# A first feed-forward product with Strassen's seven products on three of eight row-block pairs

## Chip, cores and metric

The kernel runs on one core of one Trainium2 chip. The metric is device time in microseconds (us), the median of several runs. A profiled execution has a span of its own, which is shown beside the median.

## What is computed

One layer of a streaming encoder over 256 tokens of width 2048, in float32. The change concerns the feed-forward part, the product before it (`merged @ w_o`) and the one behind it (`w_ple_gate`). D_FF is 5632.

```python
def reference(x, p, g_mix, w_in, ..., w_o, g_ffn, w_ffn_in, w_ffn_out, g_ple, w_ple_gate, w_ple_proj, g_final):
    ...
        x = x + merged @ w_o[i]

        h = rms_norm(x, g_ffn[i])
        a, b = jnp.split(h @ w_ffn_in[i], 2, axis=-1)
        x = x + (jax.nn.silu(a) * b) @ w_ffn_out[i]

        ple_gate = jax.nn.sigmoid(rms_norm(x, g_ple[i]) @ w_ple_gate[i])
        x = x + ple_gate * (p[i] @ w_ple_proj[i])
    return rms_norm(x, g_final)
```

## The kernel before

The 256 tokens are two token tiles t of 128 partitions (NT = 2, P = 128, S = 256). Each product of the layer is a stream of weight tiles from HBM. `load` (L170) has SyncE (SP) fetch four row blocks of 128 by 512 columns, 1 MB, into a `raw` tile. `split` (L185) makes of each half of it, 128x1024, a high part in the matmul's reduced float32 form on ScalarE (`hi`, L191) and the rest on VectorE (`lo`, L192). `products` (L196) then adds three matmuls of 128x512 on TensorE: high by high (L200), high by low (L201), low by high (L202). The activations on the other side are held transposed, split the same way by `transposed_split` (L144): transposes on TensorE (L137), high part on ScalarE (L152, or L159 with a gain), low part on VectorE (L153, L160).

`project` (L204) is the loop: it takes two PSUM banks, one for each token tile, and goes over the row blocks in groups of four: 24 matmuls for each group, and after each group `group_done` lets work start that was put off with `later`, so that transposes come some 24 matmuls after their inputs.

The feed-forward part is: for each of 11 blocks n of 512 columns, `fa` (the first half of w_ffn_in, 96 matmuls), its gate with sigmoid on ScalarE (L553) and a multiplication on VectorE (L554), `fb` (the second half, 96 matmuls), and the second multiplication (L559) that gives `sa`; its transposes, `aT`, come 24 matmuls into the next block. After all 11 blocks the second product `fo` runs in four column blocks over all 44 row blocks of `aT`, 264 matmuls each, and its two banks are added to x1 (L578). Ahead of it `wo` ends in the additions at L537; `pg` (w_ple_gate) comes behind it.

Order within an engine is set by the scheduler from the program's text; buffers come from pools that live as long as the kernel: `blk` (36 tiles), `raw` (4), `split` (3 pairs), and 4 + 4 PSUM banks. Since the pools are shared, loads and splits of the next product run ahead of the end of the one before.

## Time and profile before

| | |
|---|---|
| median of 3 runs | 2221.39 us (2221.09 to 2222.83) |
| span of the profiled execution | 2220.6 us |
| TensorE busy | 2205.8 us, 99% of the span |
| VectorE busy | 1222.5 us, 55% |
| ScalarE busy | 975.4 us, 44% |
| first feed-forward product (fa, fb) | 1378.9 to 1867.4 us of the span |
| second (fo) | 1867.4 to 2110.6 us |

In the profile PE is TensorE's matmuls, PEld its weight loads, DVE VectorE, ACT ScalarE, SPq the queue of SyncE, which issues the loads. A matmul's record (about 390 ns) is longer than the distance of two matmuls, since they are pipelined; the distance is what counts for time. PEclk is the granted clock of TensorE, 1.00 for 2.4 GHz and 0.50 for 1.2 GHz.

### The profile page before, as it was taken

The numbers are of one execution on the slowest core, as the hardware profiler recorded it, in microseconds if no ns is written. First come the engines' busy times: TensorE is split into PE (matmuls) and PEld (weight loads), VectorE is DVE, ScalarE is ACT, GpSimd is POOL, SyncE is SP. The second block draws the span as 40 slices with busy tenths as digits, with TensorE's granted clock in tenths as the row PEclk, the third lists the DMA queues.
The fourth block names the chain that finished last, engine by engine and source line by source line (L and its number), as shares of the span: only waits on it lengthen the run. The fifth ranks groups of instructions, "written<-read, shape, count | busy, mean of one in ns | idle before, by whom it ended". The sixth has DMA issues, their size and how long they took to land.

```text
span 2220.6 us, 24771 instructions
## 1 busy us (share of the span) xinstructions
PE 2205.8 (99%) x10054; PEld 1834.0 (83%) x10054; DVE 1222.5 (55%) x1347; ACT 975.4 (44%) x1101; POOL 9.4 (0%) x19
## 2 busy tenths in 40 slices
...
GB/s 263 187 189 190 189 189 190 195 199 193 174 190 182 181 179 186 178 178 180 177 190 189 190 209 205 185 190 192 191 184 191 191 190 183 196 194 191 191 195 128
DMA packets 229106, 420.05 MB, mean 189 GB/s; under 512 B 7424, under 2 KB 42368, under 8 KB 228992
## 3 DMA queue, kind: packets, MB, share of 16 engines
...
## 4 chain that ended last, share of the span: by engine, by line
PE 99%; DMA 0%; ACT 0%; issue 0%; DVE 0%; SPq 0%; ACTq 0%; POOLq 0%
PE fo_ps L201 4%; PE fa_ps L202 4%; PE fa_ps L201 4%; PE fa_ps L200 4%; PE fo_ps L202 4%; PE fb_ps L200 4%; PE fo_ps L200 4%; PE fb_ps L202 4%; PE fb_ps L201 4%; PE v_ps L202 3%; PE v_ps L201 3%; PE v_ps L200 3%; PE g_ps L202 3%; PE g_ps L201 3%; PE g_ps L200 3%; PE qk_ps L201 3%
## 5 line engine op out<-in xcount | busy, mean ns | idle before, releaser
L192 DVE TENSOR_TENSOR fo_lo<-fo_raw,fo_hi 128x1024 fp32r<-128x1024 f32 x88 | 107.8, 1225 | 123.5 <-ACT fo_hi L191 123.5
L192 DVE TENSOR_TENSOR fa_lo<-fa_raw,fa_hi 128x1024 fp32r<-128x1024 f32 x88 | 107.8, 1225 | 111.4 <-ACT fa_hi L191 111.4
L192 DVE TENSOR_TENSOR fb_lo<-fb_raw,fb_hi 128x1024 fp32r<-128x1024 f32 x88 | 107.8, 1225 | 110.8 <-ACT fb_hi L191 110.8
L191 ACT CAST fa_hi<-fa_raw 128x1024 fp32r<-128x1024 f32 x88 | 92.8, 1054 | 142.8 <-PE fa_ps L202 87.9
L191 ACT CAST fo_hi<-fo_raw 128x1024 fp32r<-128x1024 f32 x88 | 92.8, 1055 | 137.4 <-PE fo_ps L202 132.4
L191 ACT CAST fb_hi<-fb_raw 128x1024 fp32r<-128x1024 f32 x88 | 92.7, 1053 | 121.9 <-PE fb_ps L202 85.3
L201 PE MATMUL fo_ps<-fo_lo,aT_hi 128*128 128x512 f32 x352 | 137.1, 389 | 0.0
L202 PE MATMUL fa_ps<-fa_hi,h2T_lo 128*128 128x512 f32 x352 | 137.0, 389 | 0.0
L201 PE MATMUL fa_ps<-fa_lo,h2T_hi 128*128 128x512 f32 x352 | 137.0, 389 | 0.0
L202 PE MATMUL fo_ps<-fo_hi,aT_lo 128*128 128x512 f32 x352 | 137.0, 389 | 0.0
L201 PE MATMUL fb_ps<-fb_lo,h2T_hi 128*128 128x512 f32 x352 | 136.9, 389 | 0.0
L202 PE MATMUL fb_ps<-fb_hi,h2T_lo 128*128 128x512 f32 x352 | 136.9, 389 | 0.0
L200 PE MATMUL fa_ps<-fa_hi,h2T_hi 128*128 128x512 f32 x352 | 127.2, 392 | 0.0
L200 PE MATMUL fo_ps<-fo_hi,aT_hi 128*128 128x512 f32 x352 | 124.4, 390 | 0.0
L192 DVE TENSOR_TENSOR ro_lo<-ro_raw,ro_hi 128x1024 fp32r<-128x1024 f32 x64 | 78.4, 1225 | 83.0 <-ACT ro_hi L191 83.0
L200 PE MATMUL fb_ps<-fb_hi,h2T_hi 128*128 128x512 f32 x352 | 122.6, 389 | 0.0
L191 ACT CAST g_hi<-g_raw 128x1024 fp32r<-128x1024 f32 x64 | 67.2, 1050 | 109.8 <-PE g_ps L202 81.9
L191 ACT CAST v_hi<-v_raw 128x1024 fp32r<-128x1024 f32 x64 | 67.4, 1054 | 106.3 <-PE v_ps L202 53.3
L192 DVE TENSOR_TENSOR v_lo<-v_raw,v_hi 128x1024 fp32r<-128x1024 f32 x64 | 78.3, 1224 | 62.4 <-ACT v_hi L191 62.4
L191 ACT CAST ro_hi<-ro_raw 128x1024 fp32r<-128x1024 f32 x64 | 67.5, 1054 | 102.3 <-PE ro_ps L202 98.9
L192 DVE TENSOR_TENSOR qk_lo<-qk_raw,qk_hi 128x1024 fp32r<-128x1024 f32 x64 | 78.3, 1224 | 61.0 <-ACT qk_hi L191 61.0
L192 DVE TENSOR_TENSOR g_lo<-g_raw,g_hi 128x1024 fp32r<-128x1024 f32 x64 | 78.3, 1224 | 60.4 <-ACT g_hi L191 60.4
(241 smaller groups left out, 5467.9 us busy)
## 6 DMA issues: line engine op xcount, KB each, us to landing
fa_raw<-in_w_ffn_in_dram SPq DMA_DIRECT2D x44, 1024.0 KB, 4.9
fb_raw<-in_w_ffn_in_dram SPq DMA_DIRECT2D x44, 1024.0 KB, 4.9
fo_raw<-in_w_ffn_out_dram SPq DMA_DIRECT2D x44, 1024.0 KB, 5.0
qk_raw<-in_w_in_dram SPq DMA_DIRECT2D x64, 512.0 KB, 4.3
v_raw<-in_w_in_dram SPq DMA_DIRECT2D x32, 1024.0 KB, 5.0
g_raw<-in_w_in_dram SPq DMA_DIRECT2D x32, 1024.0 KB, 4.8
ro_raw<-in_w_ret_out_dram SPq DMA_DIRECT2D x32, 1024.0 KB, 5.0
cv_raw<-in_w_in_dram SPq DMA_DIRECT2D x16, 1024.0 KB, 4.9
```

The costliest lines, as they stand in the source:

```text
L191: last_copy[0] = nc.scalar.copy(out=hi, in_=raw[:, h0 : h0 + 2, :])
L192: nc.vector.tensor_tensor(out=lo, in0=raw[:, h0 : h0 + 2, :], in1=hi.bitcast(F32), op=ALU.subtract)
L200: nc.tensor.matmul(out=ps, lhsT=xh[:, ts], rhs=wh, start=first, stop=False)
L201: nc.tensor.matmul(out=ps, lhsT=xh[:, ts], rhs=wl, start=False, stop=False)
L202: nc.tensor.matmul(out=ps, lhsT=xl[:, ts], rhs=wh, start=False, stop=last)
```

## The change

The first product is written on pairs of row blocks. For row blocks (2i, 2i + 1), the two token tiles and the two column blocks (the `a` one and the `b` one of n) form a product of 2x2 blocks. `FAST` marks three of the eight pairs, 0, 2 and 4, for which it is done by Strassen's scheme in Winograd's form with seven block products; the other five take the plain eight. Each block product is three matmuls as before. All pairs add into the same banks P1 to P7 (the plain ones into P2 to P5), so that the scheme's closing additions are done once for each n, in `product_pair`, on VectorE. The sums on the activations' side are made once, by `pair_forms`, while `wo` runs; those on the weights' side for each fast pair: three operations on VectorE (L639, L645, L646 of the changed kernel), and then high and low parts of three blocks (1536 columns) and of four sums (2048 columns) by `halves_of` (L214 on ScalarE, L215 on VectorE).

As seven banks are taken, the second product can't wait for the end of the first with banks of its own: after every second block n it adds those two blocks' share to x1 (L742, 48 additions in all, for 8 before); the last part holds block 10 alone. The pools are closed and opened twice: ahead of the first product (`stage.open(mixed=True)`: 11 `blk`, 3 `raw`, 1 `sums`, 6 `parts` of 2048 columns, 8 PSUM banks in one pool) and behind the second. What lives across is in `keep` (20 tiles).

Counted in the built program, 9237 matmuls have 512 columns, 9336 before; those with fewer are as many as before.

```diff
+    class Stage:
+        def open(self, mixed, blks=17):
+            stage_pools.close()
+            self.mixed = mixed
+            def pool(name, bufs, **space):
+                return stage_pools.enter_context(
+                    tc.tile_pool(name=f"{name}{int(mixed)}", bufs=bufs, reuse_waits="tile", **space)
+                )
+            self.blk = pool("blk", 11 if mixed else blks)
+            if mixed:
+                self.raw = pool("raw", 3)
+                self.sums = pool("sums", 1)
+                self.parts = pool("parts", 6)
+                self.mm = self.aux = pool("ps", 8, space=PSUM)
+            else:
+                self.raw = pool("raw", 4)
+                self.split = pool("split", 3)
+                self.mm = pool("ps_mm", 4, space=PSUM)
+                self.aux = pool("ps_aux", 4, space=PSUM)
+    stage = Stage()
+    stage.open(mixed=False)
...
+    def halves_of(src, j0, jn, name):
+        hi, lo = (stage.parts.tile([P, 4, W], F32R, tag="part", name=f"{name}_{x}") for x in ("hi", "lo"))
+        last_copy[0] = nc.scalar.copy(out=hi[:, :jn, :], in_=src[:, j0 : j0 + jn, :])
+        nc.vector.tensor_tensor(
+            out=lo[:, :jn, :], in0=src[:, j0 : j0 + jn, :], in1=hi[:, :jn, :].bitcast(F32), op=ALU.subtract
+        )
+        return hi, lo
...
+        if stage.mixed:
+            hi, lo = halves_of(raw, 0, kn, name)
+            return [(hi[:, j, :], lo[:, j, :]) for j in range(kn)]
...
+    def pair_forms(src, j0, fast, name, gain):
+        pt = transposed(src, j0, f"{name}_t")
+        a = blk([P, 2, S], F32, f"{name}_a")
+        for j in range(2):
+            g = gains[:, gain + j0 + j : gain + j0 + j + 1]
+            nc.scalar.activation(out=a[:, j, :], in_=pt[:, j, :], func=AF.Copy, scale=g)
+        main = keep([P, 2, 2, S], F32R, f"{name}_f")
+        nc.scalar.copy(out=main[:, 0], in_=a)
+        nc.vector.tensor_tensor(out=main[:, 1], in0=a, in1=main[:, 0].bitcast(F32), op=ALU.subtract)
+        t1, t2 = slice(0, P), slice(P, 2 * P)
+        n = 4 if fast else 2
+        mix = blk([P, n, P], F32, f"{name}_m")
+        if fast:
+            a11, a12, a21, a22 = a[:, 0, t1], a[:, 1, t1], a[:, 0, t2], a[:, 1, t2]
+            stt = nc.vector.scalar_tensor_tensor
+            stt(out=mix[:, 0, :], in0=a21, scalar=-1.0, in1=a22, op0=ALU.mult, op1=ALU.subtract)
+            stt(out=mix[:, 1, :], in0=mix[:, 0, :], scalar=-1.0, in1=a11, op0=ALU.mult, op1=ALU.subtract)
+            nc.vector.tensor_tensor(out=mix[:, 2, :], in0=a11, in1=a21, op=ALU.subtract)
+            nc.vector.tensor_tensor(out=mix[:, 3, :], in0=a12, in1=mix[:, 1, :], op=ALU.subtract)
+        else:
+            nc.vector.tensor_tensor(out=mix, in0=a[:, :, t1], in1=a[:, :, t2], op=ALU.subtract)
+        more = keep([P, 2, n, P], F32R, f"{name}_d")
...
+    FAST = (True, False, True, False, True, False, False, False)
+    def product_pair(lhs, w, c1, c2, name):
+        banks, left = {}, {}
+        for p in range(1, 8):
+            plain = {2: 1, 3: 1, 4: 1, 5: 1}.get(p, 0)
+            left[p] = sum(3 if f else 6 * plain for f in FAST)
+        total = dict(left)
+        def add(p, stat, mov):
+            if p not in banks:
+                banks[p] = stage.mm.tile([P, W], F32, tag="ps", name=f"{name}_p{p}")
+            (xh, xl), (wh, wl) = stat, mov
+            for x, y in ((xh, wh), (xh, wl), (xl, wh)):
+                nc.tensor.matmul(out=banks[p], lhsT=x, rhs=y, start=left[p] == total[p], stop=left[p] == 1)
+                left[p] -= 1
+        c = [blk([P, NT, W], F32, f"{name}_c{i}") for i in range(2)]
+        keep_ps = blk([P, 2, W], F32, f"{name}_k")
+        us = blk([P, 2, W], F32, f"{name}_u")
+        p1, p5 = keep_ps[:, 0, :], keep_ps[:, 1, :]
+        tt = nc.vector.tensor_tensor
+        for i, fast in enumerate(FAST):
+            rows = w[2 * i * P : 2 * (i + 1) * P, :].rearrange("(c p) n -> p c n", p=P)
+            raw = stage.raw.tile([P, 4, W], F32, tag="raw", name=f"{name}_raw{i}")
+            nc.sync.dma_start(out=raw[:, 1:3, :], in_=rows[:, :, c1 : c1 + W])
+            nc.sync.dma_start(out=raw[:, 0:4:3, :], in_=rows[:, :, c2 : c2 + W])
+            if fast:
+                hi, lo = halves_of(raw, 1, 3, f"{name}_b{i}")
+                b = {k: (hi[:, j, :], lo[:, j, :]) for j, k in enumerate((1, 2, 3))}
+                sums = stage.sums.tile([P, 4, W], F32, tag="sums", name=f"{name}_s{i}")
+                tt(
+                    out=sums[:, 0:2, :],
+                    in0=raw[:, 1:4:2, :],
+                    in1=raw[:, 0:1, :].broadcast_to([P, 2, W]),
+                    op=ALU.subtract,
+                )
+                tt(out=sums[:, 2, :], in0=raw[:, 3, :], in1=sums[:, 0, :], op=ALU.add)
+                tt(out=sums[:, 3, :], in0=raw[:, 2, :], in1=sums[:, 2, :], op=ALU.subtract)
+                hi, lo = halves_of(sums, 0, 4, f"{name}_t{i}")
+                b |= {k: (hi[:, j, :], lo[:, j, :]) for j, k in enumerate((5, 7, 6, 4))}
+                for p in (1, 2, 3, 6, 7, 4, 5) if i == 0 else (1, 6, 7, 4, 5, 3, 2):
+                    add(p, lhs[i][p], b[p])
+            else:
+                hi, lo = halves_of(raw, 0, 4, f"{name}_b{i}")
+                b12, b11, b21, b22 = ((hi[:, j, :], lo[:, j, :]) for j in range(4))
+                for (a1, a2, d), (b1, b2) in zip(lhs[i], ((b11, b12), (b21, b22))):
+                    for p, stat, mov in ((4, a2, b1), (5, a2, b2), (3, d, b2), (2, a1, b1)):
+                        add(p, stat, mov)
+            if left[1] == 0 and fast:
+                nc.scalar.copy(out=p1, in_=banks[1])
+                tt(out=us[:, 0, :], in0=banks[6], in1=p1, op=ALU.add)
+                tt(out=us[:, 1, :], in0=banks[7], in1=us[:, 0, :], op=ALU.add)
+            if i < len(FAST) - 1:
+                group_done()
+        nc.scalar.copy(out=p5, in_=banks[5])
+        tt(out=c[0][:, 1, :], in0=banks[4], in1=us[:, 1, :], op=ALU.add)
+        tt(out=c[1], in0=us, in1=p5.unsqueeze(1).broadcast_to([P, 2, W]), op=ALU.add)
+        tt(out=c[1][:, 0, :], in0=banks[3], in1=c[1][:, 0, :], op=ALU.add)
+        tt(out=c[0][:, 0, :], in0=banks[2], in1=p1, op=ALU.add)
+        group_done()
+        return c
...
+    def turn_pairs(n, xn):
+        for j in range(2):
+            h2F.append(pair_forms(xn, 2 * j, FAST[2 * n + j], f"h2F{n}_{j}", G_FFN + 4 * n))
+        rows2.add(xn, n)
...
-        later(1, partial(turn_x, n, xn, rows2, G_FFN, h2T, "h2T"))
...
+    stage.open(mixed=True)
     rows3 = RowScale("r3")
+    NF = D_FF // W
+    parts_of_ff = [range(n, min(n + 2, NF)) for n in range(0, NF, 2)]
+    for part in parts_of_ff:
+        aT = {}
+        def turn_a(n, a, aT):
+            aT[n] = transposed_split(a, f"aT{n}")
+        for n in part:
+            a, b = product_pair(h2F, w_ffn_in[0], n * W, D_FF + n * W, f"f{n}")
+            if n == 0:
+                r2 = rows2.done()
+            sa = blk([P, NT, W], F32, f"sa{n}")
+            for t in range(NT):
+                nc.scalar.activation(out=sa[:, t, :], in_=a[:, t, :], func=AF.Sigmoid, scale=r2[t])
+                nc.vector.scalar_tensor_tensor(
+                    out=sa[:, t, :], in0=a[:, t, :], scalar=r2[t], in1=sa[:, t, :], op0=ALU.mult, op1=ALU.mult
+                )
+                nc.vector.scalar_tensor_tensor(
+                    out=sa[:, t, :], in0=b[:, t, :], scalar=r2[t], in1=sa[:, t, :], op0=ALU.mult, op1=ALU.mult
+                )
+            later(1, partial(turn_a, n, sa, aT))
+        last_part = part is parts_of_ff[-1]
+        for c0 in range(0, D // W, 2):
+            ps = {
+                (c, t): stage.mm.tile([P, W], F32, tag="ps", name=f"fo{part[0]}_{c}_ps{t}")
+                for c in (c0, c0 + 1)
+                for t in range(NT)
+            }
+            for n in part:
+                for c in (c0, c0 + 1):
+                    raw = load([(w_ffn_out[0], c * W, W)], n * KG, KG, f"fo{n}_{c}")
+                    ws = split(raw, KG, f"fo{n}_{c}")
+                    if n not in aT:
+                        group_done()
+                    for j in range(KG):
+                        for t in range(NT):
+                            products(
+                                ps[c, t], aT[n][j], ws[j], t, n == part[0] and j == 0, n == part[-1] and j == KG - 1
+                            )
+                    group_done()
+            for c in (c0, c0 + 1):
+                for t in range(NT):
+                    nc.vector.tensor_tensor(out=x1[c][:, t, :], in0=ps[c, t], in1=x1[c][:, t, :], op=ALU.add)
+                if last_part:
+                    later(1, partial(turn_x, c, x2[c], rows3, G_PLE, h3T, "h3T"))
+    stage.open(mixed=False, blks=17)
+    group_done()
```

VectorE at the end of `wo` and the start of the first product. Before (names: `x1_3` is the last column block of x1, `fa0_lo` a low part of the first product's weights):

```order
L192 TENSOR_TENSOR fa0_lo0_9885<-fa0_raw_9882,fa0_hi0_9884 128x1024
L192 TENSOR_TENSOR fa0_lo2_9889<-fa0_raw_9882,fa0_hi2_9888 128x1024
L537 TENSOR_TENSOR x1_3_9877<-wo3_ps0_9715,res3_9713 128x512
L537 TENSOR_TENSOR x1_3_9877<-wo3_ps1_9716,res3_9713 128x512
L192 TENSOR_TENSOR fa0_lo0_9943<-fa0_raw_9940,fa0_hi0_9942 128x1024
L255 TENSOR_REDUCE ssum_10042<-r2_parts_9218 128x2
```

and in the changed kernel (`f0_s0` are the sums of pair 0 of block 0, `f0_b0` its blocks' parts, `f0_t0` the parts of its sums, `r2` and `rms` the row scale):

```order
L690 TENSOR_TENSOR x1_3_9925<-wo3_ps1_9749,res3_9746 128x512
L295 TENSOR_REDUCE ssum_10268<-r2_parts_9221 128x2
L265 TENSOR_SCALAR rms_v_10270<-ssum_10268 128x2
L267 TENSOR_SCALAR rms_h_10271<-rms_v_10270 128x2
L271 TENSOR_TENSOR rms_e_10273<-rms_h_10271,rms_y_10272 128x2
L272 TENSOR_TENSOR rms_e_10273<-rms_e_10273,rms_y_10272 128x2
L273 SCALAR_TENSOR_TENSOR r2_r_9222<-rms_e_10273,rms_y_10272 128x2
L639 TENSOR_TENSOR f0_s0_9961<-f0_raw0_9954 128x1024
L645 TENSOR_TENSOR f0_s0_9961<-f0_raw0_9954,f0_s0_9961 128x512
L215 TENSOR_TENSOR f0_b0_lo_9958<-f0_raw0_9954,f0_b0_hi_9957 128x1536
L646 TENSOR_TENSOR f0_s0_9961<-f0_raw0_9954,f0_s0_9961 128x512
L215 TENSOR_TENSOR f0_t0_lo_9966<-f0_s0_9961,f0_t0_hi_9965 128x2048
```

Of the first product's splits, two stood ahead of the last additions to x1 and one right behind; now all stand behind them, and SyncE issues the load of `f0_raw0` only after the last one, for which it waits.

VectorE after the first product's block 1. Before, the two multiplications that end `sa1` stand between splits of the next product:

```order
L192 TENSOR_TENSOR fa2_lo2_10507<-fa2_raw_10500,fa2_hi2_10506 128x1024
L559 SCALAR_TENSOR_TENSOR sa1_10353<-fb1_ps0_10358,r2_r_9219,sa1_10353 128x512
L559 SCALAR_TENSOR_TENSOR sa1_10353<-fb1_ps1_10359,r2_r_9219,sa1_10353 128x512
L192 TENSOR_TENSOR fa2_lo0_10553<-fa2_raw_10550,fa2_hi0_10552 128x1024
L192 TENSOR_TENSOR fa2_lo2_10557<-fa2_raw_10550,fa2_hi2_10556 128x1024
L192 TENSOR_TENSOR fa2_lo0_10587<-fa2_raw_10584,fa2_hi0_10586 128x1024
L153 TENSOR_TENSOR aT1_lo_10535<-aT1_t0_10536,aT1_hi_10534 128x512
L153 TENSOR_TENSOR aT1_lo_10535<-aT1_t2_10543,aT1_hi_10534 128x512
```

and in the changed kernel, where block 1 is followed by the second product's part of blocks 0 and 1 (`f1_c0`, `f1_c1` are the two results, `f1_p2` to `f1_p4` banks, `f1_u` and `f1_k` partial sums):

```order
L664 TENSOR_TENSOR f1_c0_10287<-f1_p4_10326,f1_u_10290 128x512
L665 TENSOR_TENSOR f1_c1_10288<-f1_u_10290,f1_k_10289 128x1024
L667 TENSOR_TENSOR f1_c0_10287<-f1_p2_10310,f1_k_10289 128x512
L713 SCALAR_TENSOR_TENSOR sa1_10585<-f1_c0_10287,r2_r_9222,sa1_10585 128x512
L666 TENSOR_TENSOR f1_c1_10288<-f1_p3_10314,f1_c1_10288 128x512
L716 SCALAR_TENSOR_TENSOR sa1_10585<-f1_c1_10288,r2_r_9222,sa1_10585 128x512
L215 TENSOR_TENSOR fo1_0_lo_10675<-fo1_0_raw_10672,fo1_0_hi_10674 128x2048
L713 SCALAR_TENSOR_TENSOR sa1_10585<-f1_c0_10287,r2_r_9222,sa1_10585 128x512
L716 SCALAR_TENSOR_TENSOR sa1_10585<-f1_c1_10288,r2_r_9222,sa1_10585 128x512
L215 TENSOR_TENSOR fo1_1_lo_10705<-fo1_1_raw_10702,fo1_1_hi_10704 128x2048
L181 TENSOR_TENSOR aT1_lo_10627<-aT1_t0_10628,aT1_hi_10626 128x512
```

Four additions and the gate's four operations now stand behind the product, with a low part of 2048 columns between the first token tile's gate and the second's; the transposes for `aT1` wait for the last one.

TensorE at the end of the last block, 10. Before:

```order
L200 MATMUL fb10_ps1_13050<-fb10_hi2_13159,h2T3_hi_9916 128x512
L201 MATMUL fb10_ps1_13050<-fb10_lo2_13160,h2T3_hi_9916 128x512
L202 MATMUL fb10_ps1_13050<-fb10_hi2_13159,h2T3_lo_9917 128x512
L200 MATMUL fo0_ps0_13191<-fo0_hi0_13195,aT0_hi_10235 128x512
L200 MATMUL fo0_ps1_13192<-fo0_hi0_13195,aT0_hi_10235 128x512
L201 MATMUL fo0_ps0_13191<-fo0_lo0_13196,aT0_hi_10235 128x512
L202 MATMUL fo0_ps0_13191<-fo0_hi0_13195,aT0_lo_10236 128x512
L201 MATMUL fo0_ps1_13192<-fo0_lo0_13196,aT0_hi_10235 128x512
```

and in the changed kernel:

```order
L620 MATMUL f10_p2_14351<-f10_b7_lo_14578,h2F3_1_f_10021 128x512
L620 MATMUL f10_p2_14351<-f10_b7_hi_14577,h2F3_1_f_10021 128x512
L165 MATMUL aT10_t0_14629<-ident_83,sa10_14610 128x128 x4
L165 MATMUL aT10_t2_14636<-ident_83,sa10_14610 128x128 x4
L240 MATMUL fo10_0_ps0_14617<-fo10_0_hi_14623,aT10_hi_14627 128x512
L241 MATMUL fo10_0_ps0_14617<-fo10_0_lo_14624,aT10_hi_14627 128x512
L240 MATMUL fo10_0_ps1_14618<-fo10_0_hi_14623,aT10_hi_14627 128x512
L241 MATMUL fo10_0_ps1_14618<-fo10_0_lo_14624,aT10_hi_14627 128x512
```

Before, the second product began with `aT0`, ready since long, and the transposes of `aT10` stood 24 matmuls further on; now they stand between the last matmul of block 10 and the first of its second product, which reads `aT10`.

## Rows read from the trace of the kernel before

**Rows 1.** The page's part 1: engine, busy us (share of the span), instructions.

```profile
PE 2205.8 (99%) x10054; PEld 1834.0 (83%) x10054; DVE 1222.5 (55%) x1347; ACT 975.4 (44%) x1101; POOL 9.4 (0%) x19
```

**Rows 2.** Waits of TensorE, whole run: us in total, times, longest.

```profile
PE cc_ps L200 <- ACT hT_hi L159: 4.2, 1, 4.2
PE warm_ps L130 <- POOL ident masks.py:199: 1.4, 1, 1.4
```

**Rows 3.** Windows in fa/fb and fo: length, busy by engine, PEclk, DMA share, GB/s.

```profile
1401.00:1890.00 489.00, 489.00 (x2204) 405.88 (x2203) 259.37 (x243) 210.05 (x220) 0.00 (x0) 1.00 0.55 189
1890.00:2135.00 245.00, 245.00 (x1100) 203.14 (x1100) 120.77 (x119) 107.05 (x124) 0.69 (x1) 1.00 0.57 193
```

**Rows 4.** Timeline of ScalarE in fa: start, duration, operation, [idle before <-releaser].

```profile
1426.20 1.05 ACT L191 CAST fa_hi<-fa_raw 128x1024 fp32r<-128x1024 f32 x1 [1.66 <-PE fa_ps L202]
1428.92 1.05 ACT L191 CAST fa_hi<-fa_raw 128x1024 fp32r<-128x1024 f32 x1 [1.67 <-PE fa_ps L202]
...
1432.53 1.05 ACT L191 CAST fa_hi<-fa_raw 128x1024 fp32r<-128x1024 f32 x1 [1.59 <-PE fa_ps L202]
```

**Rows 5.** VectorE by line and shape: busy us, mean ns | idle before, releaser.

```profile
L192 DVE TENSOR_TENSOR fa_lo<-fa_raw,fa_hi 128x1024 fp32r<-128x1024 f32 x88 | 107.8, 1225 | 111.4 <-ACT fa_hi L191 111.4
...
L554 DVE SCALAR_TENSOR_TENSOR sa<-fa_ps,r_r,sa 128x512 f32<-128x512 f32 x22 | 15.7, 751 | 5.0 <-ACT sa L553 5.0
L559 DVE SCALAR_TENSOR_TENSOR sa<-fb_ps,r_r,sa 128x512 f32<-128x512 f32 x22 | 15.4, 743 | 0.0
L153 DVE TENSOR_TENSOR aT_lo<-aT_t,aT_hi 128x512 fp32r<-128x512 f32 x22 | 14.1, 682 | 0.0
```

**Rows 6.** ScalarE by line and shape, the same columns.

```profile
L191 ACT CAST fa_hi<-fa_raw 128x1024 fp32r<-128x1024 f32 x88 | 92.8, 1054 | 142.8 <-PE fa_ps L202 87.9 <-PE fb_ps L202 50.0 <-PE wo_ps L202 4.9
...
L246 ACT ACTIVATE junk<-x 128x512 f32<-128x512 f32 x22 | 13.9, 633 | 2.2 <-DVE x L589 1.9
...
L152 ACT CAST aT_hi<-aT_t 128x512 fp32r<-128x512 f32 x22 | 11.7, 584 | 0.0
...
L159 ACT ACTIVATE h3T_hi<-h3T_t,gains 128x256 fp32r<-128x256 f32 x16 | 6.8, 471 | 3.8 <-DVE h3T_lo L160 3.8
...
L347 ACT CAST ych<-y 128x512 fp32r<-128x512 f32 x8 | 4.9, 622 | 0.4
```

**Rows 7.** Timeline of VectorE in fa, operations in a queue.

```profile
1421.85 1.22 DVE L192 TENSOR_TENSOR fa_lo<-fa_raw,fa_hi 128x1024 fp32r<-128x1024 f32 x1 [1.49 <-ACT fa_hi L191]
1422.99 1.40 DVE L559 SCALAR_TENSOR_TENSOR sa<-fb_ps,r_r,sa 128x512 f32<-128x512 f32 x2
```

**Rows 8.** Timeline of the first product's start, where TensorE waits.

```profile
9.92 1.22 DVE L192 TENSOR_TENSOR cc_lo<-cc_raw,cc_hi 128x1024 fp32r<-128x1024 f32 x1 [4.58 <-ACT cc_hi L191]
...
10.32 1.22 PE L200 MATMUL cc_ps<-cc_hi,hT_hi 128*128 128x512 f32 x2 [4.17 <-ACT hT_hi L159]
...
11.20 0.50 PEld L201 LDWEIGHTS cc_ps<-cc_lo,hT_hi 128*128 128x128 f32 x2 [0.38 <-DVE cc_lo L192]
11.34 1.09 PE L201 MATMUL cc_ps<-cc_lo,hT_hi 128*128 128x512 f32 x2
```

**Rows 9.** DMA issues: count, KB each, median us from issue to landing.

```profile
fa_raw<-in_w_ffn_in_dram SPq DMA_DIRECT2D x44, 1024.0 KB, 4.9
...
qk_raw<-in_w_in_dram SPq DMA_DIRECT2D x64, 512.0 KB, 4.3
...
cc_raw<-in_w_in_dram SPq DMA_DIRECT2D x8, 512.0 KB, 9.8
```

**Rows 10.** Windows at the start and at the end, columns as in rows 3.

```profile
10.00:13.00 3.00, 2.68 (x6) 1.89 (x7) 3.00 (x5) 2.43 (x5) 0.00 (x0) 0.50 1.05 399
13.00:16.00 3.00, 3.00 (x14) 2.75 (x13) 1.73 (x5) 1.83 (x4) 0.00 (x0) 0.67 1.05 391
...
2210.00:2215.00 5.00, 1.32 (x12) 1.12 (x10) 1.82 (x7) 1.20 (x4) 0.55 (x1) 1.00 0.00 0
2215.00:2221.00 6.00, 0.00 (x0) 0.00 (x0) 0.93 (x2) 1.11 (x2) 0.00 (x0) 0.63 0.48 175
```

More of the change, by code (lines that the diff above doesn't have):

```diff
@@ L204, in project @@
     def project(lhs, nk, pieces, name, loaded=None, before=None):
-        ps = [ps_mm.tile([P, W], F32, tag="mm", name=f"{name}_ps{t}") for t in range(NT)]
+        ps = [stage.mm.tile([P, W], F32, tag="ps", name=f"{name}_ps{t}") for t in range(NT)]
         for k0 in range(0, nk, KG):
```

100 lines of the change are left out of this document (41 added, 59 removed).

## Prediction

> **What bounds the kernel now.** I read the engines' busy time first: TensorE is busy 2205.8 of 2220.6 us [rows 1]. Then TensorE's waits: two in the whole run, 4.2 and 1.4 us, both at the start [rows 2]. Then the two feed-forward stretches: in both TensorE is busy to the last hundredth at a granted clock of 1.00, VectorE about half of the time [rows 3]. So a matmul that goes away is worth its full pitch, and every wait that appears on TensorE costs its full length. The pitch is read from ScalarE, which TensorE paces there: its splits come 2.72 us apart for 12 matmuls, 0.2267 us each; with the eight transposes of a finished block between them 3.61 us, so eight transposes cost 0.89 [rows 4]. The profiled execution spans 2220.6 us; the median is 0.8 more, and I add that at the end.
>
> **What is removed.** A fast pair takes 7 x 3 = 21 matmuls for 24; three of eight pairs are fast, so a column block n takes 183 for 192. Over 11 blocks 99 are gone: 99 x 0.2267 = **-22.4 us**. The second product keeps its 1056.
>
> **What VectorE gets.** From 512 columns (682 ns) to 1024 (1225) it takes 1.061 ns a column [rows 5], so an operation of 1536 columns takes 1.77 us and one of 2048 2.31. A fast pair asks for 1.77 (low part of the blocks), 1.23 + 0.68 + 0.68 (sums) and 2.31 (low part of the sums) = 6.67; a plain pair for 2.31. A block n: 3 x 6.67 + 5 x 2.31 + 4.63 (six evictions) + 3.0 (the two gates) + 1.4 (aT) = 40.6 us, some 2.6 less because operations in a queue overlap by about 0.08 [rows 7]. TensorE needs 183 x 0.2267 + 0.89 = 42.4. VectorE still fits on average, but with little to spare. In the Trainium skill, VectorE: DVE Perf Modes (the TRN2 errata), a float32 tensor_tensor goes as (N + 151) / 0.96 ns: for 1024 columns 1224, with which the row of 1225 agrees. By it 2048 columns would be 2.29, an estimate from the page; the sum would fall by about 0.3 us.
>
> ScalarE goes from 622 to 1054 ns for 512 more columns [rows 6], so 1.49 us for 1536 and 1.92 for 2048: 3 x 3.41 + 5 x 1.92 and a few small ones, about 24 us of 42.4, hidden behind TensorE except at the seams below.
>
> **The hand-over into every odd block.** The 7 banks are evicted into the start of the next product. I lay VectorE's queue out in its order, at 0.08 overlap; t = 0 is the last matmul of block n - 1. The additions out of the banks end at 1.69 (line 665) and 2.29 (667), the gate at 2.95, a sum of the next fast pair at 3.55, the last eviction at 4.15, and only then the low part of plain pair 1, to 6.38. A waiting matmul starts 0.2 us after VectorE's end (9.92 + 1.22 = 11.14, load 11.20, matmul 11.34 [rows 8]). TensorE wants it after 21 matmuls, one high one and eight transposes: 4.76 + 0.23 + 0.89 = 5.88. Stall 0.70. Pair 5 comes at 28.29 + 0.2 for 27.86: 0.63. Together 1.34; five odd blocks: **+6.7 us**. From both sides: nothing, if the dozen queued operations are 0.06 us shorter each, and 2.0 a block, if 0.06 longer. Even blocks begin after the second product, where VectorE was idle half of the time [rows 3]: laid out the same way they show no stall.
>
> **From the odd block to the second product.** The transposes of the odd block's gate stand 24 matmuls (5.44 us) behind the product's end. On VectorE the low part of the next weights, 2.31, stands between the two token tiles' gates: end of the second 6.75, + 0.2. Stall 1.5, five times: **+7.5 us** (0.9 to 2.1 each: 4.5 to 10.5).
>
> **The seam into the first block.** Before, loads and splits of the first block ran ahead of the last add of w_o. Now the mixed stage's first load waits for it: the second add ends about 0.75 us after the last matmul, SP issues from 0.95 on, two loads that take some 0.5 to issue and 4.3 to 4.9 to land [rows 9]; landed at 6.4 (5.9 to 8.5; the same kind of load took 9.8 in the crowd at the start). Then in line: 1.15 + 0.6 + 1.7 + 0.6 on VectorE, t_hi 1.92 on ScalarE, t_lo 2.3: 14.75, + 0.2. By then 13 matmuls (2.9) have run in the gaps: 12.0 lost. VectorE is still behind at pairs 1 and 2, by 0.4 and 1.5. **+13.9 us** (12 to 17). The rest of w_o's forms, the sums of squares and h2F3 are covered by this hole.
>
> **The last block alone.** Block 10 is a part of its own, so nothing stands between it and its second product: evictions, gates (6.75), transposes, aT_hi (584 ns each, [rows 6]), first matmul at 8.3; less the eight transposes (0.89): **+7.4 us** (6.4 to 8.4). Its aT_lo and the four weight splits are covered: the splits were made ahead.
>
> **The seam out of it.** On ScalarE the first w_ple_gate split stands behind two squares (0.63 and its read-out, about 0.82 each), eight h3T forms (0.47 each), and pT_hi; it is over at about 7.1, its low part and the 0.2 at 8.5. Two matmuls (0.45) and 20 transposes (2.2) run meanwhile: **+5.8 us** (4.8 to 7). The 48 evictions of the second product for 8, 40 x 0.68, lie on VectorE in the second product beside full TensorE and cost nothing; without that cover they'd cost 27.
>
> **The clock.** After the idle 4.17 us at the start the granted clock was 0.50 (the lower level, 1.2 GHz) over 10 to 13 us and 0.67 over 13 to 16 [rows 10]: 1.3 + 1.0 = 2.3 us lost. But at the end it was still 1.00 in a stretch with 1.32 us of work in five. Three seams of 6 to 12 us each cost 0 to 2.3; I take half, 1.2, as much of it falls where TensorE waits anyhow: **+3.6 us** (0 to 7).
>
> Sum: -22.4 + 6.7 + 7.5 + 13.9 + 7.4 + 5.8 + 3.6 = +22.5; 2220.6 + 22.5 + 0.8 = **2243.9**, say 2244. All lower ends together give 2227, all upper ends about 2260.
>
> **Rivals.** (1) *Not slower: the pitch falls.* Matmuls now go round seven banks. If that lowers the pitch in the first product's 2013 matmuls from 0.2267 to 0.2155 us, it returns 22.5 us: 2221; to 0.2130, 2216. Against it: the 12 matmuls in 2.72 us change their bank every third one, as a plain pair still does. 10%, four of it within 0.2%. In the Trainium skill, TensorE: Matmul & The Clock Gate (Back-to-back issue gap), 512 columns cost 215.7 ns; our row shows 226.7, so the measurement decides.
> (2) *The hand-overs are covered.* Both stalls of the odd blocks hang on 0.5 to 1.5 us in a queue; if they vanish, 14.2 go: 2230 (2223 to 2232). 15%.
> (3) *VectorE becomes the bound.* If the sums' high part on ScalarE (1.92) leaves VectorE waiting in each fast pair, a block takes 40.6 + 3 x 1.92 = 46.4 rather than 42.4. Half of that, less the 6.7 already counted, makes +15: 2259; all of it 2281. Against: other low parts stand between the sums and t_lo in steady state. 10%.
> (4) *The short holes lower the clock too.* 15 of them, at up to 2.3: 2250 to 2278. For it: 4.17 us was enough at the start; against: no row shows it for 0.6 to 1.5 us. 6%. In the Trainium skill, TensorE: Matmul & The Clock Gate (A second HAM failure mode), short idle times between groups of matmuls make the clock swing; by it this case would have the larger share. No run here shows it yet.
> (5) *The matmuls aren't dropped.* The built program has 99 fewer; if time follows something else, +22.4: 2266. 2%.
>
> **How the numbers follow.** Forecast 2244 (2231 to 2258): 57%. With rivals 2 to 4 in part the range 2224 to 2268 leaves out about 2 in 10. A measurement tells 0.2%, 4.4 us, from no change. Faster: 6% (rival 1). Same: 4% of rival 1 and 3% of rival 2, 7%. Slower: 87%.
>
> **What would show it.** TensorE's waits: 12 us in front of f0's first pair, released by the load, then VectorE; 7 before fo10's first matmul, released by ScalarE; 5 to 6 before pg0; 0.6 to 0.7 twice in odd blocks; 1.5 before five transposes of aT, released by VectorE. An even block should take 42.4 us. A first load issued before w_o's last add, odd blocks as short as even ones, or a split of the first 1 MB on time would prove the sum wrong.

## Result

The changed kernel takes 2242.71 us (2241.46 to 2244.32 in four runs) against 2221.24 for the kernel before: a ratio of 1.0098, interval 1.0083 to 1.0112. It is slower by 1%, though 99 matmuls are gone. The forecast was 2244 in 2224 to 2268. The profiled execution of the changed kernel spans 2242.5 us, 21.9 more than that of before.

The page of the changed kernel, part 1, against [rows 1]:

```profile
PE 2199.7 (98%) x9955; PEld 1820.0 (81%) x9955; DVE 1414.2 (63%) x1470; ACT 1015.0 (45%) x1040; POOL 9.4 (0%) x19
```

VectorE has 192 us more to do, TensorE is busy only 6 us less. Where TensorE waits is the answer to [rows 2] (us in total, times, longest):

```profile
PE aT_t L165 <- DVE sa L716: 13.3, 6, 6.8
PE f_p L620 <- ACT f_b_hi L214: 8.8, 3, 7.6
PE f_p L620 <- DVE f_b_lo L215: 3.8, 6, 1.2
PE pT_t L165 <- issue: 1.9, 1, 1.9
PE pg_ps L240 <- ACT pg_hi L231: 1.7, 1, 1.7
PE warm_ps L158 <- POOL ident masks.py:199: 1.4, 1, 1.4
PE cc_ps L240 <- ACT cc_hi L231: 1.3, 1, 1.3
PE cc_ps L241 <- DVE cc_lo L232: 0.5, 1, 0.5
```

Two waits have become eight kinds. Three of them (warm_ps and the two of cc_ps) stand at the kernel's start, as both did before. The others are in places that the prediction named: six waits for the gate (five of 1.3 and one of 6.8), one of 7.6 ahead of the first block, short ones for a low part in the odd blocks, and those ahead of w_ple_gate. One releaser differs: at block 10 the long wait stands before the transposes and VectorE's gate ends it, where the prediction named ScalarE and the first matmul behind them. What ended the 1.9 us before pT ("issue") the profile does not show. The new operations on VectorE cost what was worked out for them (by line and shape, as in [rows 5]):

```profile
L215 DVE TENSOR_TENSOR fo_lo<-fo_raw,fo_hi 128x2048 fp32r<-128x2048 f32 x44 | 100.8, 2291 | 65.1 <-ACT fo_hi L214 65.1
L215 DVE TENSOR_TENSOR f_t_lo<-f_s,f_t_hi 128x2048 fp32r<-128x2048 f32 x33 | 75.6, 2292 | 40.9 <-ACT f_t_hi L214 40.9
L215 DVE TENSOR_TENSOR f_b_lo<-f_raw,f_b_hi 128x1536 fp32r<-128x1536 f32 x33 | 57.9, 1754 | 15.5 <-ACT f_b_hi L214 15.5
```

2.29 and 1.75 us for the 2.31 and 1.77 of the straight line through two rows. In the Trainium skill, VectorE: DVE Perf Modes (the TRN2 errata), the rule (N + 151) / 0.96 gives 2.29 and 1.76 as an estimate; the trace agrees. The two ways differ by at most 0.02 us for an operation.

The sum of the prediction beside what the trace gives. Each measured entry is a distance between first and last matmuls of stages on TensorE's timeline, less their matmuls at 0.2267 us and their transposes at 0.111 (the profiles of before and of the changed kernel, one each):

| step | predicted | measured |
|---|---|---|
| 99 matmuls fewer | -22.4 | -22.4 |
| odd blocks, five | +6.7 | +8.0 |
| gate before the second product, five | +7.5 | +7.7 |
| seam into block 0 | +13.9, and a third of the clock | +14.1 |
| block 10 alone, and its second product at a low clock | +7.4, and a third of the clock | +7.8 and +1.8 |
| seam into w_ple_gate | +5.8, and a third of the clock | +7.4 |
| the clock itself | +3.6 | in the three entries above |
| the kernel's head, and its end | 0 | -2.3 and -0.3 |
| sum | +22.5 | +21.9 |

Three of the odd blocks cost 1.3 us each, blocks 1 and 9 cost 2.0 and 2.1. The entries are rounded; their sum is that of the unrounded ones.

The seam into block 0, from the timeline of the changed kernel (start, duration, operation, idle time and releaser):

```profile
1376.06 1.37 DVE L690 TENSOR_TENSOR x<-wo_ps,res 128x512 f32<-128x512 f32 x2 [5.17 <-PE wo_ps L242]
...
1377.51 0.37 SPq L632 DMA_DIRECT2D f_raw<-in_w_ffn_in_dram  x1
...
1382.79 1.23 DVE L639 TENSOR_TENSOR f_s<-f_raw 128x1024 f32<-128x1024 f32 x1 [2.78 <-DMA f_raw<-in_w_ffn_in_dram]
...
1384.30 1.22 PE L620 MATMUL f_p<-f_b_hi,h2F_f 128*128 128x512 f32 x2 [7.60 <-ACT f_b_hi L214]
...
1389.04 2.29 DVE L215 TENSOR_TENSOR f_t_lo<-f_s,f_t_hi 128x2048 fp32r<-128x2048 f32 x1 [2.02 <-ACT f_t_hi L214]
```

w_o's last matmul is through at 1376.55. The second addition ends at 1377.43, SyncE issues at 1377.51, the load is there 6.2 us after the last matmul (6.4 was forecast), and the last low part of pair 0 ends at 1391.33, 14.8 us after it (14.75).

The clock (windows, columns as in [rows 3]; the granted clock is the third number from the end):

```profile
1384.30:1392.50 8.20, 7.68 (x19) 5.50 (x20) 6.18 (x5) 5.39 (x5) 0.00 (x0) 0.50 0.77 267
1392.60:1430.00 37.40, 36.22 (x160) 29.18 (x159) 30.54 (x27) 19.36 (x17) 0.00 (x0) 1.00 0.60 199
1430.00:2048.00 618.00, 607.59 (x2699) 497.85 (x2698) 474.10 (x378) 285.08 (x199) 0.00 (x0) 1.00 0.57 192
2098.90:2102.50 3.60, 3.60 (x10) 2.83 (x10) 1.33 (x2) 0.59 (x1) 0.00 (x0) 0.50 0.00 0
2130.80:2136.60 5.80, 5.76 (x13) 4.07 (x14) 3.45 (x3) 1.81 (x2) 0.00 (x0) 0.50 1.04 382
```

Behind each of the three seams TensorE begins at the lower level, 1.2 GHz. Across 618 us between the first and the second, with some fifteen short waits of at most 1.3 us, it is never granted less than 2.4 GHz.

### The profile page after: what moved, and what is told of

The parts are those of the page before. It is cut to its first block, busy times and chain, and to the rows that moved or that the text cites. A ratio compares the mean times of both kernels' runs of the same rounds, so it can differ in the third digit from the quotient of the medians.

```text
span 2242.5 us, 24813 instructions
## 1 busy us (share of the span) xinstructions
PE 2199.7 (98%) x9955; PEld 1820.0 (81%) x9955; DVE 1414.2 (63%) x1470; ACT 1015.0 (45%) x1040; POOL 9.4 (0%) x19
## 4 chain that ended last, share of the span: by engine, by line
PE 90%; DVE 6%; ACT 2%; issue 1%; DMA 1%; SPq 0%; ACTq 0%; POOLq 0%; DVEq 0%
PE f_p L620 14%; PE fo_ps L240 3%; PE fo_ps L241 3%; PE fo_ps L242 3%; PE v_ps L242 3%; PE v_ps L241 3%; PE g_ps L242 3%; PE v_ps L240 3%; PE g_ps L241 3%; PE g_ps L240 3%; PE ro_ps L241 3%; PE qk_ps L241 3%; PE qk_ps L242 3%; PE ro_ps L242 3%; PE qk_ps L240 3%; PE ro_ps L240 3%
## 5 line engine op out<-in xcount | busy, mean ns | idle before, releaser
L620 PE MATMUL f_p<-f_b_hi,h2F_f 128*128 128x512 f32 x792 | 274.0, 391 | 7.6 <-ACT f_b_hi L214 7.6
L215 DVE TENSOR_TENSOR f_b_lo<-f_raw,f_b_hi 128x1536 fp32r<-128x1536 f32 (+1 forms) x88 | 183.3, 2086 | 34.8 <-ACT f_b_hi L214 34.4
L214 ACT CAST f_b_hi<-f_raw 128x1536 fp32r<-128x1536 f32 (+1 forms) x88 | 152.1, 1751 | 103.6 <-PE f_p L620 53.5
L620 PEld LDWEIGHTS f_p<-f_b_hi,h2F_f 128*128 128x128 f32 x792 | 149.3, 189 | 38.4 <-ACT f_b_hi L214 8.0
L620 PE MATMUL f_p<-f_b_lo,h2F_f 128*128 128x512 f32 x396 | 156.4, 395 | 4.4 <-DVE f_b_lo L215 3.8
L214 ACT CAST fo_hi<-fo_raw 128x2048 fp32r<-128x2048 f32 x44 | 84.0, 1910 | 140.6 <-PE fo_ps L241 61.0
L215 DVE TENSOR_TENSOR fo_lo<-fo_raw,fo_hi 128x2048 fp32r<-128x2048 f32 x44 | 100.8, 2291 | 65.1 <-ACT fo_hi L214 65.1
L231 ACT CAST v_hi<-v_raw 128x1024 fp32r<-128x1024 f32 x64 | 67.5, 1054 | 106.3 <-PE v_ps L242 53.4
L231 ACT CAST ro_hi<-ro_raw 128x1024 fp32r<-128x1024 f32 x64 | 67.5, 1054 | 102.3 <-PE ro_ps L242 98.9
L620 PE MATMUL f_p<-f_b_hi,h2F_d 128*128 128x512 f32 x286 | 112.4, 393 | 1.2 <-ACT f_b_hi L214 1.2
L214 ACT CAST f_t_hi<-f_s 128x2048 fp32r<-128x2048 f32 x33 | 63.1, 1913 | 109.1 <-DVE f_s L646 68.4
L215 DVE TENSOR_TENSOR f_t_lo<-f_s,f_t_hi 128x2048 fp32r<-128x2048 f32 x33 | 75.6, 2292 | 40.9 <-ACT f_t_hi L214 40.9
L241 PE MATMUL v_ps<-v_lo,hT_hi 128*128 128x512 f32 x256 | 100.6, 393 | 0.0
```

Source lines behind the costliest of these rows:

```text
L214: last_copy[0] = nc.scalar.copy(out=hi[:, :jn, :], in_=src[:, j0 : j0 + jn, :])
L215: nc.vector.tensor_tensor(out=lo[:, :jn, :], in0=src[:, j0 : j0 + jn, :], in1=hi[:, :jn, :].bitcast(F32), op=ALU.subtract)
L231: last_copy[0] = nc.scalar.copy(out=hi, in_=raw[:, h0 : h0 + 2, :])
L241: nc.tensor.matmul(out=ps, lhsT=xh[:, ts], rhs=wl, start=False, stop=False)
L620: nc.tensor.matmul(out=banks[p], lhsT=x, rhs=y, start=left[p] == total[p], stop=left[p] == 1)
```

## Experiments

Each of them starts from the changed kernel unless it says otherwise.

**1. The load earlier.** What holds the first load back is where its buffer lies: on a tile that w_o's last additions read. With the pools in another order it lies on tiles that are long free.

```diff
-            self.blk = pool("blk", 11 if mixed else blks)
             if mixed:
+                self.sums = pool("sums", 1)
                 self.raw = pool("raw", 3)
-                self.sums = pool("sums", 1)
                 self.parts = pool("parts", 6)
...
+            self.blk = pool("blk", 11 if mixed else blks)
```

> Only the places of the mixed stage's buffers differ: the first loads lie where tiles have long been free, so they are issued before the last additions of w_o. Theory (the seam is a wait for the load and then a chain on VectorE that the row scale's six small operations hold back until 3.5 us after the last matmul): the first block's chain starts at 3.5 instead of 6.2, the stretch from w_o's last matmul to the second product goes from 101.1 to 98.3 us, the whole 2240 us. Rival (the load alone makes the seam): at least the 6.2 us go, 2236 or less. Rival (the clock or something else makes it): 2242 to 2243.

2241.78 us, 0.9 less, which lies within the spread of the four runs: by the whole time alone the last rival (2242 to 2243) would do as well. The stretch decides. From w_o's last matmul to the second product it went from 101.1 to 97.5 us, by 3.6 rather than 2.8: 2.9 from the earlier start of the chain, and 0.7 because block 1 waited 0.35 us for a low part where the changed kernel's profile has 1.06. In this profile w_o's last matmul comes 2.1 later (1378.4 for 1376.3), by the kernel's head, which hides most of that in the whole. VectorE's timeline of this kernel:

```profile
1378.16 1.37 DVE L691 TENSOR_TENSOR x<-wo_ps,res 128x512 f32<-128x512 f32 x2 [5.17 <-PE wo_ps L243]
1380.40 0.16 DVE L296 TENSOR_REDUCE ssum<-r_parts 128x2 f32<-128x8 f32 x1 [0.86 <-ACT junk L287]
...
1381.56 0.16 DVE L272 TENSOR_TENSOR rms_e<-rms_h,rms_y 128x2 f32<-128x2 f32 x1 [0.60 <-POOL rms_y L267]
...
1382.03 1.22 DVE L640 TENSOR_TENSOR f_s<-f_raw 128x1024 f32<-128x1024 f32 x1
```

No wait for a load is left, and yet the sums begin 3.4 us after the last matmul (1378.65): the row scale, which nobody needs before the end of block 0, stands in front and waits for ScalarE and GpSimd. The rival of the load alone falls; the last one falls by the stretch, not by the time.

**2. And the row scale later.** On top of experiment 1, the row scale and the last sums of squares are queued behind block 0's splits.

```diff
-        rows2.add(xn, n)
+        with tc.issue_after(last_copy[0].ins):
+            rows2.add(xn, n)
...
-                r2 = rows2.done()
+                with tc.issue_after(lows[-1].ins):
+                    r2 = rows2.done()
```

> As e1_load, and the row scale and the last sums of squares queue behind the first block's splits. Theory: the chain on VectorE starts right after the two additions, at 0.8 us; the stretch goes from 101.1 to about 95.7, the whole to 2237 us. Rival (the load alone): the same as e1_load.

2238.88 us; the stretch takes 95.1 us, 6.0 less than in the changed kernel, of which the time shows 3.8: w_o's last matmul starts 2.0 later in this profile (1378.3 for 1376.3), by the kernel's head, which the edit does not touch. What remains of the seam, about 9 us, is the chain of sums and low parts on VectorE and the splits on ScalarE between them, which have no matmuls beside them yet, and a lower clock behind the wait of 3.6 us in it (0.50 from 1386 to 1390).

**3. The gates first.** The first low part of an odd block's w_ffn_out weights is queued behind the gates of both token tiles (`gates` holds their last operations).

```diff
...
-                    ws = split(raw, KG, f"fo{n}_{c}")
+                    if len(part) > 1 and n == part[1] and c == 0:
+                        with tc.issue_after(gates[0].ins), tc.issue_after(gates[1].ins):
+                            ws = split(raw, KG, f"fo{n}_{c}")
...
```

> Only the order on VectorE differs: behind an odd block the first low part of that block's w_ffn_out weights comes after both token tiles' gates instead of between them. Theory (the transposes wait 1.5 us for the second gate, which stands behind that low part): the wait goes five times, each second product's part takes 44.4 instead of 45.95 us, the whole 2235. Rival (the low part is needed as early as the gate): the wait comes back 48 matmuls later, 2241 to 2243.

2235.56 us. TensorE's wait for the gate is now only that of block 10:

```profile
PE aT_t L165 <- DVE sa L717: 6.8, 1, 6.8
```

Each part of the second product takes 44.4 us from its first matmul to the next block's, 45.95 before; nothing came back 48 matmuls later.

**4. No fast pair.**

```diff
-    FAST = (True, False, True, False, True, False, False, False)
+    FAST = (False,) * 8
```

(The closing additions that have nothing to add are left out, and two banks are only copied, on VectorE.)

> All eight pairs plain, so 192 matmuls for a block again, no weight sums and three evictions of 512 columns fewer on VectorE; stages, buffers and parts as in the changed kernel. Theory (99 matmuls are worth their pitch, 22.4 us, and the stalls of odd blocks come from VectorE's load with the sums): +22.4, less 7.3 for the odd blocks, 3.5 for a shorter first seam, 1.5 to 5 for a shorter end of a block: 2249 us (2245 to 2255); a pair of blocks takes 88 to 89 us. Rival (time does not follow the matmuls): 2228 to 2235.

2250.77 us. A pair of blocks takes 87.9 us, which is its 384 matmuls and eight transposes and no wait at all; in the window of such a pair (columns as in [rows 3]) TensorE is busy without a gap and VectorE half of the time:

```profile
1522.20:1610.10 87.90, 87.90 (x393) 72.89 (x392) 44.39 (x29) 34.48 (x23) 0.00 (x0) 1.00 0.56 191
```

In the changed kernel it takes 85.2. So 18 matmuls fewer, 4.1 us, return 2.8: the odd blocks' stall of 1.3 is the price of the sums. And the stages and parts alone, with no saving, cost 29 us; of their 22.4 us the three fast pairs return 8 against that.

**5. Four and five fast pairs.** The edit is that of four; five are pairs 0, 2, 3, 5 and 6.

```diff
-    FAST = (True, False, True, False, True, False, False, False)
+    FAST = (True, False, True, False, True, False, True, False)
```

> Four fast pairs (0, 2, 4, 6) instead of three: 180 matmuls for a block, 33 fewer in all (7.5 us), and 4.36 us more on VectorE for each block. Theory (VectorE is nearly full): its queue asks for about 42.2 us of a block against 41.7 on TensorE, so the gain is eaten: a pair of blocks takes 85 to 87 us (85.2 with three), the whole 2242 to 2253. Rival (TensorE still sets the pace): 83.4 + 1.3, the whole 2235.

2277.39 us: far beyond both. The first product itself is shorter (84.5 us a pair of blocks), as the rival would have it (83.4 + 1.3). But the second product's part takes 51.8 instead of 45.95:

```profile
PE aT_t L165 <- DVE sa L716: 32.1, 6, 7.5
PE f_p L620 <- ACT f_b_hi L214: 15.6, 10, 7.3
```

```profile
1536.20:1620.70 84.50, 83.42 (x371) 68.52 (x370) 76.79 (x62) 46.75 (x33) 0.00 (x0) 1.00 0.56 191
1620.70:1672.50 51.80, 46.92 (x199) 38.64 (x198) 32.33 (x28) 17.25 (x13) 0.00 (x0) 0.93 0.51 175
```

In the first window VectorE is busy 76.8 of 84.5 us. In the second the transposes wait 4.9 us for the gate, five times, where the changed kernel has 1.3. VectorE's queue behind an odd block:

```profile
1622.94 2.28 DVE L215 TENSOR_TENSOR fo_lo<-fo_raw,fo_hi 128x2048 fp32r<-128x2048 f32 x1
...
1627.73 2.28 DVE L215 TENSOR_TENSOR fo_lo<-fo_raw,fo_hi 128x2048 fp32r<-128x2048 f32 x1
1629.93 0.74 DVE L716 SCALAR_TENSOR_TENSOR sa<-f_c,r_r,sa 128x512 f32<-128x512 f32 x1
```

Two low parts of w_ffn_out's weights stand here between the end of the block and its last gate operation; in the changed kernel it is one. VectorE has also worked without a gap since 1610.5. The last gate operation ends 10.0 us after the block's last matmul, in the changed kernel 6.9. Behind such a wait the clock goes down as well (0.93 over the window). My expectation had the direction, but looked for the price in the first product and so missed its size. How much of it is VectorE's load and how much the order in its queue was not tried.

> Five fast pairs (0, 2, 3, 5, 6): 177 matmuls for a block and 8.7 us more on VectorE. Theory: VectorE is the bound, about 46.3 us a block: a pair of blocks takes 92 to 97 us, the whole 2280 to 2310. Rival (TensorE sets the pace): 2228.

2345.82 us, above the range. A pair of blocks takes 104.2 us, more than the 92 to 97 expected, and VectorE is busy only 86.0 of them (the third busy time of the window below). TensorE waits for the sums' high part on ScalarE, while neighbouring fast pairs leave no other work between; and the granted clock over the pair of blocks is 0.92:

```profile
PE f_p L620 <- ACT f_t_hi L214: 51.0, 22, 3.3
```

```profile
1544.70:1648.80 104.10, 91.89 (x365) 71.76 (x364) 86.04 (x71) 49.54 (x35) 0.00 (x0) 0.92 0.48 164
```

This is the mechanism of the prediction's third rival. With three fast pairs and a plain one behind each it does not show; with more it does.

**6. The two late seams.** The last part holds blocks 8 to 10, its last two columns run one after the other, and h3T3, the last squares and pT queue behind the first splits of w_ple_gate.

```diff
-    parts_of_ff = [range(n, min(n + 2, NF)) for n in range(0, NF, 2)]
+    parts_of_ff = [range(n, n + 2) for n in range(0, NF - 3, 2)] + [range(NF - 3, NF)]
...
-        for c0 in range(0, D // W, 2):
+        for cs in ((0, 1), (2,), (3,)) if last_part else ((0, 1), (2, 3)):
...
-                    later(1, partial(turn_x, c, x2[c], rows3, G_PLE, h3T, "h3T"))
+                    later(1, partial(turn_late if c == 3 else turn_x, c, x2[c], rows3, G_PLE, h3T, "h3T"))
...
-    group_done()
...
-        pT.extend(transposed_split(p_in, "pT", wide=PLE))
+        with tc.issue_after(last_copy[0].ins):
+            pT.extend(transposed_split(p_in, "pT", wide=PLE))
```

> The last part holds blocks 8 to 10 instead of 10 alone, its last two columns run one after the other, and the forms of the last column queue behind the first splits of w_ple_gate. Theory (the two late seams are waits for a chain that had nothing beside it): the wait of 6.8 us before aT10 becomes one of 1.5, with no lower clock behind it (-8.1); in front of w_ple_gate 4.5 to 5 us go: 2230 (2227 to 2233). Rival (what is uncovered moves on): the blocks wait for buffers in the part of three, and 2238 or more.

2228.01 us, 14.7 less; how that divides among the changes was not tried. No wait of more than 1.3 us is left before a transpose of aT, and the wait before w_ple_gate is gone:

```profile
PE f_p L620 <- ACT f_b_hi L214: 8.6, 3, 7.3
PE aT_t L165 <- DVE sa L720: 5.2, 4, 1.3
PE f_p L620 <- DVE f_b_lo L215: 3.6, 9, 1.0
```

**7. The fast pairs spread.**

```diff
-    FAST = (True, False, True, False, True, False, False, False)
+    FAST = (True, False, False, True, False, True, False, False)
```

> Three fast pairs as before, but 0, 3 and 5 instead of 0, 2 and 4; the work is the same. Theory (the odd blocks' stalls come from sums and low parts crowded into the first pairs): the second stall of an odd block (0.6) goes, the first stays or shrinks, and pair 2 of block 0 loses its 1.5: a pair of blocks 84.2 to 84.8 instead of 85.2, the whole 2238 (2235 to 2242). Rival (VectorE's total alone decides): no change, 2242 to 2243.

2250.96 us, 8 more than the changed kernel; both theories fall. (Only the stretch up to the second product gained, 98.5 us for 101.1.) At an odd block's start the sum of the next fast pair stands in VectorE's queue ahead of pair 1's low part, as it does in the changed kernel, but here that pair is one further on, its load is one later in a ring of three buffers, and VectorE waits for it with pair 1's low part behind:

```profile
1567.74 1.22 DVE L639 TENSOR_TENSOR f_s<-f_raw 128x1024 f32<-128x1024 f32 x1 [0.78 <-DMA f_raw<-in_w_ffn_in_dram]
...
1571.35 2.28 DVE L215 TENSOR_TENSOR f_b_lo<-f_raw,f_b_hi 128x2048 fp32r<-128x2048 f32 x1
```

That is the smaller part of what TensorE loses there. The larger wait is for ScalarE's high part of the fast pair (its 1536 columns), since in this program one matmul of pair 3 stands on TensorE's queue ahead of pair 1's low products:

```profile
1571.05 1.47 ACT L214 CAST f_b_hi<-f_raw 128x1536 fp32r<-128x1536 f32 x1 [0.41 <-ACT sa L712]
```

```profile
1572.58 0.50 PE L620 MATMUL f_p<-f_b_hi,h2F_f 128*128 128x512 f32 x1 [1.16 <-ACT f_b_hi L214]
1573.68 0.50 PE L620 MATMUL f_p<-f_b_lo,h2F_f 128*128 128x512 f32 x1 [0.60 <-DVE f_b_lo L215]
```

The work is the same and so is its total. What decides the odd blocks here is what the queues' order puts in front, and whether that is ready.

**8. All mends together.** Experiments 2, 3 and 6 in one kernel.

> The mends of e1_first, e2_gate and e6_seam in one kernel; the products, fast pairs and sums are those of the changed kernel. Theory (the seams and the second gate are separate prices beside a saving of 22.4 us): they add up, -6.0 - 7.6 - 14.7 of 2242.7: 2214.5 (2212 to 2218), 0.3% under the kernel before. Rival (VectorE's backlog only moves): 2220 or more.

2216.31 us, a ratio to the kernel before of 0.9973, interval 0.9962 to 0.9984: faster than both. The savings add up (2242.7 - 3.8 - 7.2 - 14.7 = 2217.0), and the waits of the new stages that remain are the chain of block 0's first pairs and the odd blocks:

```profile
PE f_p L624 <- DVE f_b_lo L218: 5.9, 8, 3.6
PE cc_ps L244 <- ACT cc_hi L235: 1.5, 1, 1.5
```

**9. The sums behind the low part before them**, on top of experiment 8.

```diff
+                with tc.issue_after(lows[-2].ins) if i else ExitStack():
...
-                tt(out=sums[:, 2, :], in0=raw[:, 3, :], in1=sums[:, 0, :], op=ALU.add)
-                tt(out=sums[:, 3, :], in0=raw[:, 2, :], in1=sums[:, 2, :], op=ALU.subtract)
+                    tt(out=sums[:, 2, :], in0=raw[:, 3, :], in1=sums[:, 0, :], op=ALU.add)
+                    tt(out=sums[:, 3, :], in0=raw[:, 2, :], in1=sums[:, 2, :], op=ALU.subtract)
```

> As e8_all, and on VectorE the sums of a fast pair queue behind the low part of the pair before it, so that plain pair 1 of an odd block is ready some 1 us earlier. Theory (VectorE's queue at an odd block's start is a backlog, so that what is taken from pair 1 falls on pair 2, whose sums end at about 15 us instead of 13): nothing gained or some lost against e8_all, 2214 to 2222. Rival (only the order is wrong): 0.7 us for each odd block, about 2211.

2230.20 us: 14 lost, more than the theory's bound. Pair 1 no longer waits, but a pair of blocks takes 87.7 us instead of 85.1. ScalarE now waits for the sums, and the next pair's high part queues behind the sums' high part:

```profile
PE f_p L624 <- ACT f_b_hi L217: 14.7, 16, 1.3
```

```profile
1572.11 1.91 ACT L217 CAST f_t_hi<-f_s 128x2048 fp32r<-128x2048 f32 x1 [6.88 <-DVE f_s L651]
...
1574.63 1.90 ACT L217 CAST f_b_hi<-f_raw 128x2048 fp32r<-128x2048 f32 x1
```

**10. Two fast pairs**, on top of experiment 8.

```diff
-    FAST = (True, False, True, False, True, False, False, False)
+    FAST = (True, False, True, False, False, False, False, False)
```

> As e8_all with two fast pairs (0 and 2) instead of three: 33 matmuls more (7.5 us), 4.36 us less on VectorE for each block. Theory (a fast pair returns its 0.68 us of TensorE a block only while VectorE has room, and the stall at pair 5 of odd blocks, 0.6, is the third pair's price): a pair of blocks takes 85.8 us (85.1 with three), the whole 2219 to 2222. Rival (the third pair costs the odd blocks their whole stall): 85.2, the whole 2216 to 2217.

2225.34 us, above both ranges. A pair of blocks takes 85.9 us, as expected: the third fast pair still returns 0.8 for the 1.4 of its six matmuls, 3.3 us over all blocks. The rest of the 9 us, between 5 and 6, is a wait that has nothing to do with the pairs, and the lower clock behind it (0.50 from 2111 to 2113, 0.70 from there to 2118): in this program SyncE issued w_ple_gate's first load at 2105.48, after the second product, and not some five microseconds ahead of its end as in experiment 8, and ScalarE, and TensorE behind it, waited for it:

```profile
2110.55 1.99 ACT L235 CAST pg_hi<-pg_raw 128x1024 fp32r<-128x1024 f32 x2 [14.45 <-DMA pg_raw<-in_w_ple_gate_dram]
```

```profile
PE pg_ps L244 <- ACT pg_hi L235: 4.1, 1, 4.1
```

What held it there was not tried.

## Why the prediction held, point by point

- **A matmul is worth its pitch.** Shown from both sides: block 10, for which nothing else waits inside, takes 41.5 us = 183 x 0.2267, and the plain kernel's pair of blocks is its matmuls and transposes and nothing else. The even blocks take 41.5 us too, not the 42.4 that the prediction gave them: the eight transposes counted there stand in the second product, which does not touch the sum. Rival 1 (a lower pitch with seven banks) is out: the pitch in the changed kernel is 0.2267 as before.
- **VectorE fits on average, not at the hand-overs.** Confirmed for three fast pairs. Odd blocks 3, 5 and 7 lose 1.3 us each, in the two places laid out (some 0.6 at pair 1 and 0.4 at pair 5, the rest around the transposes); blocks 1 and 9 lose 0.7 and 0.8 more, which a second profile (experiment 1) does not show. At an odd block's start the trace reads (VectorE, then TensorE):

```profile
1567.74 0.69 DVE L645 TENSOR_TENSOR f_s<-f_raw,f_s 128x512 f32<-128x512 f32 x1
1568.35 0.68 DVE L666 TENSOR_TENSOR f_c<-f_p,f_c 128x512 f32<-128x512 f32 x1
1568.95 2.28 DVE L215 TENSOR_TENSOR f_b_lo<-f_raw,f_b_hi 128x2048 fp32r<-128x2048 f32 x1
```

```profile
1571.28 0.50 PE L620 MATMUL f_p<-f_b_lo,h2F_f 128*128 128x512 f32 x1 [0.35 <-DVE f_b_lo L215]
```

In this order stand the sum, the eviction, and only then the low part that TensorE waits for. But that the total of VectorE's work makes this stall, as "little to spare" suggests, is too simple: experiments 7 and 9 kept the work, changed its order and lost 8 and 14 us.
- **The gate behind a low part.** The predicted 1.5 us was measured five times, and mended by order alone (experiment 3). Rival 2 is out; both stalls stood there.
- **The seam into block 0.** The size was right, and so was the chain. That the load is the first link is right, but it is not the seam: taking it away brought the chain forward by 2.9 of 14 us, since the row scale, which the prediction took as covered by the hole, was the next thing late (experiments 1 and 2).
- **The last block alone and the seam out.** Right in size (7.8 for 7.4; 7.4 with the clock for 5.8 without), and right in what stands in line; experiment 6 took 14.7 us out of both.
- **The clock.** The three restarts cost about 1, 1.8 and 2 us, 4.8 where 3.6 stood (estimates from the matmuls behind each, which stand 0.43 us apart at the lower level for 0.2267). The term was mis-sized, within its bounds. Rival 4 is out for the waits of this kernel, which are at most 1.3 us there: the window from 1430 to 2048 shows 1.00. In the Trainium skill, TensorE: Matmul & The Clock Gate (A second HAM failure mode), short idle times between groups of matmuls make the clock swing between its levels. The trace of the changed kernel does not show that; in experiment 5 it does, with waits of up to 3.3 us close together (five pairs, 0.92 over a pair of blocks) and of 4.9 us (four pairs, 0.93).
- **What was not foreseen**: the head of the profiled execution. Its first weights were there sooner, TensorE waited 1.3 and 0.5 us there for 4.2 in [rows 2], and w_o's last matmul came at 1376.3 instead of 1378.6. It is no part of the change: in the other profiles that matmul comes anywhere from 1376.1 to 1378.7, with the code ahead of it the same in all but the fast pairs' forms. That the sum comes within 0.6 us is therefore partly luck: this return of 2.3 us stands against odd blocks and a clock that cost 1.3 and 1.2 more than forecast.

So none of the five rivals shows with three fast pairs (the fifth falls with experiment 4: without the saving the time is 8 us longer). The saving was real and the price was at the seams, where one stage's buffers or results let the next one start: they hold 31 of the table's 47 us (14.1, 7.8 + 1.8 and 7.4).
